# A run of four products per weight block, and retention's value products in runs of three key blocks

## Chip, cores and metric

The kernel runs on one core of one Trainium2 chip. The metric is the device time in microseconds (us) of one launch; its median over three runs is 3030.82 (3021.84 to 3036.25).

## What is computed

Two blocks of a network over 512 latent tokens and 256 context tokens, 1024 features each, in float32. The first block has two layers; the change touches the first layer's mixer, which is retention (eight heads of 64) beside a state-space scan. Two pieces matter here, in the reference's words.

Parameters of the modulation, from two conditioning vectors:

```
def adaln_params(cond, w_ada, b_ada):
    m = jax.nn.silu(cond) @ w_ada + b_ada
    return jnp.split(m[:, None, :], 6, axis=-1)
```

`w_ada` is 1024 x 6144. Retention, per head and direction, is a decayed attention without a softmax:

```
scores = jnp.einsum('bhnid,bhnjd->bhnij', qc, kc) * decay
y_intra = jnp.einsum('bhnij,bhnjv->bhniv', scores, vc)
```

with the state carried from chunk to chunk, forward and backward, and the latent scans starting from the context's final state. The kernel computes the same sum in one go: all 768 keys against the 512 latent queries, and the 256 context keys against the 256 context queries, each score multiplied by a decay that is a function of the distance.

## The kernel before

One program in Python emits instructions through helpers (`act` is line 382, `tt` line 390, `stt` line 393, `load` line 405), and a scheduler then sets each engine's order: of what is ready by its model it takes what stands first in the program, or in a high-priority block. SBUF is an arena whose places are taken in the order of their last release; PSUM is eight banks. All loads and spills are issued on one queue, SP, in order. The engines also work in order.

**Parameter products.** `ada(parts, w)` is called in this stage with parts 1 and 2 and w = 1. Each part is 2048 columns, in eight blocks of 128 rows of the weights. A block is four loads of 128 x 512 (256 KB each), and four products: the 32-column stationary operand holds the conditioning vectors, padded from two columns to 32, and product q writes PSUM partitions 32q to 32q + 32 of one bank (line 611). Each product follows its load, and the load's place is given back. The arena's zone 2 is 2560 floats a partition, five such places. After eight blocks come a copy, four transposes (line 620) and the sums with the bias.

**Retention.** `ret_pair` handles two heads. It first prepares `kk`, `qh` and `ql` (high and low parts of keys and queries; 64 x 768 pieces on ACT, DVE and POOL) and the decay strips `st` and `st2`. Then six key blocks J of 128: `scores` makes two products for each head (lines 1111 and 1112, 128 keys by 512 latent queries, 256 context queries too for J of 0 and 1) and multiplies them on DVE by the strip into `w`; `values` follows at once with one product per head (line 1120), 64 columns of stationary values, head i into partitions 64i to 64i + 64. The generator yields after each key block, seven times in all. `gn_center` (line 1168) and the statistics (line 1179) end the pair.

**The weave.** `mixer0` runs generators side by side: three head pairs (rate 27), the block gemms `blocks` (rate 8: the queries and keys of pairs 2 and 3, then four gate blocks; lines 435, 437 and 440), and `ada` (rate 18). Each step taken adds 1/rate to a generator's clock and the one that is furthest behind goes next; this sets the order in the program. A second weave holds the other mixer's finish (`ssd_finish`, rate 5) and the fourth pair (rate 9). After it come the norm's statistics (line 473), the finish's products and the output projection.

Float products (lines 611, 1120, 976, 1168) are two matmul instructions each in the trace; products of split operands (435, 437, 440, 1111, 1112) are one.

Of the kernel before, what the change touches and what calls it, by code (L numbers as in the profile page):

```python
# [12 lines left out]
OP = mybir.AluOpType  # L13
# [3 lines left out]
TL, TC, TA = 512, 256, 768  # L17
# [343 lines left out]
class _K:  # L361
# [19 lines left out]
    def act(self, out, in_, func=AF.Copy, **kw):  # L381
        return self.nc.scalar.activation(out, in_, func, **kw)  # L382

    def behind(self, ins, other):

        self.tc.add_manual_dep(ins.ins, other.ins.name, mybir.DependencyInfo(mybir.DependencyClass.Sync, mybir.DependencyReason.DATA),
                               reason="in one run")

    def tt(self, out, a, b, op, eng=None):
        return (eng or self.nc.vector).tensor_tensor(out, a, b, op=op)  # L390
# [208 lines left out]
    def ada(self, parts, w=2):  # L599

        nc, A, B = self.nc, self.A, self.B
        src, cs, out = self.I["wada"], self.cs, self.P[0]
        for g in parts:
            b = B.new()
            for k in range(8):
                for hf in range(4 // w):
                    c0 = g * 2048 + hf * w * 512
                    raw = self.load(src[k * 128:(k + 1) * 128, c0:c0 + w * 512])
                    for j in range(w):
                        q = w * hf + j  # L610
                        nc.tensor.matmul(b.a[32 * q:32 * q + 32, :], cs.a[:, k, :], raw.a[:, j * 512:(j + 1) * 512],  # L611
                                         start=(k == 0), stop=(k == 7))
                    raw.free()
                yield
            s = A.new([512])
            self.act(s.a, b.a)
            b.free()
            b2 = B.new()
            for nb in range(4):
                nc.tensor.transpose(b2.a[:, nb * 128:(nb + 1) * 128], s.a[:, nb * 128:(nb + 1) * 128], self.ident.a)  # L620
            s.free()
            src2 = b2.a.rearrange("p (n j v) -> p j n v", n=4, j=4)
            for v in range(2):
                self.tt(out.a[:, g * 16:(g + 1) * 16, v].rearrange("p (j n) -> p j n", j=4), src2[:, :, :, v],
                        self.bada.a[:, 0, g * 16:(g + 1) * 16].rearrange("p (j n) -> p j n", j=4), OP.add)
            b2.free()
            for q0 in (8, 32):
                if g * 16 <= q0 < g * 16 + 16:
                    nc.vector.tensor_scalar(out.a[:, q0:q0 + 8, :], out.a[:, q0:q0 + 8, :], 1.0, None, op0=OP.add)
# [442 lines left out]
    def ret_pair(self, c, pr, q, k, v):  # L1072

        nc, A, B = self.nc, self.A, self.B
        mm = nc.tensor.matmul
        la, lb, t, dst = c["la"], c["lb"], c["t"], c["dst"]
        half = [slice(0, 64), slice(64, 128)]
        if c["var"] is None:
            c["var"] = B.new()
        pyc, pvar = c["var"].a[:, :TC], c["var"].a[:, TC:TC + 48]  # L1080

        kk, qh, ql = (A.new([2, TA], F32R) for _ in range(3))
        for i in range(2):
            o, w = half[i], half[1 - i]
            self.act(kk.a[o, i, :], k.a[o])
            self.act(qh.a[o, i, :], q.a[o])
            self.act(qh.a[w, i, :], q.a[o])
            self.tt(kk.a[w, i, :], k.a[o], kk.a[o, i, :], OP.subtract, nc.gpsimd)
            self.tt(ql.a[o, i, :], q.a[o], qh.a[o, i, :], OP.subtract, nc.gpsimd)
            self.tt(ql.a[w, i, :], q.a[o], qh.a[o, i, :], OP.subtract)  # L1090
        self.free([k, q])
        st, st2, u = A.new([2, 896]), A.new([2, 640]), A.new([640])
        for i in range(2):
            h = 2 * pr + i
            nc.vector.tensor_scalar(st.a[:, i, :], dst.a, la.a[:, h:h + 1], None, op0=OP.mult)
            self.stt(st.a[:, i, :], dst.a, lb.a[:, 0, 8 + h:9 + h], st.a[:, i, :], OP.mult, OP.min)
            self.act(st2.a[:, i, :], dst.a[:, 256:896], AF.Exp, scale=la.a[:, h:h + 1], bias=lb.a[:, 1, h:h + 1])
            self.act(u.a, dst.a[:, 256:896], AF.Exp, scale=lb.a[:, 0, 8 + h:9 + h], bias=t.a[:, 8 + h:9 + h])
            self.tt(st2.a[:, i, :], st2.a[:, i, :], u.a, OP.add, nc.gpsimd)
        self.act(st.a, st.a, AF.Exp)  # L1100
        u.free()
        yield
        pyl = B.new()

        def scores(J, t0, t1, strip):
            n = t1 - t0
            p, w = B.new(2 if n > 256 else 1), A.new([2, n])
            p3 = p.a.rearrange("p (i t) -> p i t", i=2)
            js = slice(J * 128, (J + 1) * 128)
            for i in range(2):  # L1110
                mm(p3[:, i, :], kk.a[:, i, js], qh.a[:, i, t0:t1], start=True, stop=False)
                mm(p3[:, i, :], kk.a[:, i, js], ql.a[:, i, t0:t1], start=False, stop=True)  # L1112
            self.tt(w.a, p3, strip, OP.mult)
            p.free()
            return w

        def values(J, w, out, last):
            for i in range(2):
                vv = v.a[:, J, 128 * pr + 64 * i:128 * pr + 64 * i + 64]
                mm(out[half[i]], vv, w.a[:, i, :], start=(J == 0), stop=(J == last))  # L1120
            w.free()

        for J in range(6):
            if J < 2:
                strip = st2.a[:, :, 128 - 128 * J:640 - 128 * J]
            else:
                strip = st.a[:, :, 384 - 128 * (J - 2):896 - 128 * (J - 2)]
            values(J, scores(J, TC, TA, strip), pyl.a, 5)
            if J < 2:
                values(J, scores(J, 0, TC, st.a[:, :, 384 - 128 * J:640 - 128 * J]), pyc, 1)  # L1130
            yield
        self.free([st, st2, kk, qh, ql])
        yb = A.new([TA])
        self.act(yb.a[:, :TC], pyc)
        self.act(yb.a[:, TC:], pyl.a)
        pyl.free()
        self.dump("yret%d" % pr, yb.a)
        c["ds"].append(self.gn_center(yb, TA, c["center"], c["blk2"], pvar, pr))
# [1613 lines left out]
```

## Time and profile before

| what | value |
|---|---|
| median of three runs | 3030.82 us |
| profiled execution, its own time | 3028.96 us |
| its span | 3027.3 us, 43733 instructions |
| PE | 2845.5 us busy (94%), 17880 matmuls |
| DVE | 1704.7 us (56%) |
| ACT | 980.8 us (32%) |
| POOL | 298.6 us (10%) |
| line 611 | 1% of the chain that ended last |

A busy share is the time that an engine had an instruction under way. Matmuls are pipelined: one lasts longer than the distance to the next one's start, and several on separate strips of the array can be under way together, so lengths add up to more than busy time. In a timeline the distance from one start to the next start is what a piece of work takes from PE. The stage of this change lies between 290 and 460 us of the span.

### The profile page before, as it was taken

How to read it: one execution, taken by the hardware profiler on the slowest of the kernel's cores; microseconds unless marked ns; L12 is line 12 of the kernel's file. 1: busy time of each engine (PE TensorE's matmuls, PEld its weight loads, DVE VectorE, ACT ScalarE, POOL GpSimd, SP SyncE). 2: the span in 40 equal slices, each digit the busy share in tenths (PEclk: the TensorE clock that was granted, in tenths of full speed). 3: DMA queues.
4: the chain of work that ended last, by engine and by line, in shares of the span. 5: the costliest groups of instructions: out<-in, count | busy, mean ns of one | idle time of the engine just before them, and what ended most of it. 6: DMA issues, size and time to landing. Idle time of an engine off the chain costs nothing.

```text
span 3027.3 us, 43733 instructions
## 1 busy us (share of the span) xinstructions
PE 2845.5 (94%) x17880; PEld 2061.2 (68%) x17880; DVE 1704.7 (56%) x2733; ACT 980.8 (32%) x1605; POOL 298.6 (10%) x271
## 2 busy tenths in 40 slices
PE   7989999999999999999999999979799898999997
PEld 4776557888888877666698778876675664344443
DVE  5856447776576355677664782378856843121113
ACT  5522434511211146444554522254323322001011
POOL 0134310000000010122000000010311211000000
PEclk9999999999999999999999999989898888999998
DMA  6334362366465112001322222222213145999998
GB/s 220 104 108 122 122 196 76 119 212 218 140 223 202 42 66 93 21 31 42 118 70 91 91 77 77 71 84 77 71 49 105 43 147 207 398 409 409 409 409 294
DMA packets 170584, 458.98 MB, mean 152 GB/s; under 512 B 20320, under 2 KB 52704, under 8 KB 170000
## 3 DMA queue, kind: packets, MB, share of 16 engines
q1 hardware_dynamic: 170384, 456.19, 42.9%
q8 instruction: 140, 2.29, 0.3%
q14 instruction: 60, 0.49, 0.0%
HBM read 441.35 MB, written 14.78 MB: 151 GB/s over the span
## 4 chain that ended last, share of the span: by engine, by line
PE 68%; DVE 10%; DMA 5%; issue 4%; ACT 2%; POOL 1%; SPq 0%; DVEq 0%; ACTq 0%; POOLq 0%
PE ps L435 13%; PE ps L440 13%; PE ps L437 13%; PE ps L2609 9%; DVE mem L390 5%; ACT mem L382 2%; PE ps L2592 2%; PE ps L1625 1%; DVE mem L393 1%; DMA mem<-in_wadt_dram 1%; PE ps L611 1%; DMA mem<-in_ed_dram 1%; DMA mem<-in_eu_dram 1%; PE ps L1783 1%; POOL mem L390 1%
## 5 line engine op out<-in xcount | busy, mean ns | idle before, releaser
L382 ACT ACTIVATE mem<-mem 128x1024 fp32r<-128x1024 f32 (+16 forms) x802 | 543.2, 707 | 874.4 <-PE ps L440 223.3
L390 DVE TENSOR_TENSOR mem<-mem,mem 128x1024 fp32r<-128x1024 f32 (+13 forms) x595 | 507.9, 870 | 366.6 <-ACT mem L382 161.4
L382 ACT ACTIVATE mem<-ps 128x512 f32<-128x512 f32 (+8 forms) x607 | 311.9, 528 | 992.2 <-PE ps L440 334.4
L435 PE MATMUL ps<-mem,mem 128*128 128x512 f32 (+3 forms) x1991 | 597.3, 357 | 14.9 <-ACT mem L382 10.8
L437 PE MATMUL ps<-mem,mem 128*128 128x512 f32 (+2 forms) x1906 | 568.5, 354 | 1.1 <-DVE mem L390 0.9
L440 PE MATMUL ps<-mem,mem 128*128 128x512 f32 (+2 forms) x1977 | 417.6, 352 | 0.0
L435 PEld LDWEIGHTS ps<-mem,mem 128*128 128x128 f32 (+2 forms) x1991 | 338.2, 189 | 82.8 <-ACT mem L382 17.8
L437 PEld LDWEIGHTS ps<-mem,mem 128*128 128x128 f32 (+1 forms) x1906 | 325.6, 189 | 60.8 <-issue 6.7
L440 PEld LDWEIGHTS ps<-mem,mem 128*128 128x128 f32 (+1 forms) x1977 | 324.1, 190 | 56.2 <-issue 4.1
L2609 PE MATMUL ps<-mem,mem 128*64 128x512 f32 x1344 | 309.5, 599 | 1.1 <-ACT mem L382 0.3
L437 PE MATMUL ps<-mem 128*128 128x512 f32 (+1 forms) x814 | 272.5, 365 | 1.4 <-POOL mem L390 0.9
L435 PE MATMUL ps<-mem 128*128 128x512 f32 (+1 forms) x729 | 255.1, 374 | 12.4 <-ACT mem L382 8.5
L390 POOL TENSOR_TENSOR mem<-mem 128x256 f32<-128x256 f32 (+4 forms) x72 | 96.2, 1337 | 1683.5 <-ACT mem L382 1392.8
L390 DVE TENSOR_TENSOR mem<-mem,ps 128x512 f32<-128x512 f32 (+5 forms) x234 | 129.0, 582 | 203.5 <-PE ps L2609 103.5
L2609 PEld LDWEIGHTS ps<-mem,mem 128*64 128x64 f32 x1344 | 107.2, 137 | 177.9 <-issue 163.8
L390 DVE TENSOR_TENSOR mem<-mem 128x256 f32<-128x256 f32 (+19 forms) x347 | 186.4, 544 | 68.6 <-ACT mem L382 22.9
L390 POOL TENSOR_TENSOR mem<-mem,mem 128x512 f32<-128x512 f32 (+6 forms) x104 | 142.5, 1380 | 534.4 <-ACT mem L382 438.0
L390 DVE TENSOR_TENSOR mem<-ps,mem 128x512 f32<-128x512 f32 (+6 forms) x196 | 123.1, 644 | 99.1 <-PE ps L1112 35.2
L437 PEld LDWEIGHTS ps<-mem 128*128 128x128 f32 x814 | 152.8, 195 | 27.9 <-DVE mem L390 2.5
L440 PE MATMUL ps<-mem 128*128 128x512 f32 (+3 forms) x743 | 171.4, 360 | 0.0
L435 PEld LDWEIGHTS ps<-mem 128*128 128x128 f32 x729 | 139.2, 196 | 44.8 <-ACT mem L382 13.4
L393 DVE SCALAR_TENSOR_TENSOR mem<-ps,mem 128x256 f32<-128x256 f32 (+1 forms) x232 | 114.6, 533 | 76.2 <-PE ps L440 75.9
(301 smaller groups left out, 2901.7 us busy)
## 6 DMA issues: line engine op xcount, KB each, us to landing
mem<-in_eg_dram SPq DMA_DIRECT2D x128, 512.0 KB, 10.2
mem<-in_eu_dram SPq DMA_DIRECT2D x128, 512.0 KB, 10.2
mem<-in_ed_dram SPq DMA_DIRECT2D x128, 512.0 KB, 10.2
mem<-in_wadt_dram SPq DMA_DIRECT2D x96, 512.0 KB, 4.3
mem<-in_wup_dram SPq DMA_DIRECT2D x44, 512.0 KB, 3.6
mem<-in_wgate_dram SPq DMA_DIRECT2D x44, 512.0 KB, 3.5
mem<-in_wdown_dram SPq DMA_DIRECT2D x40, 512.0 KB, 3.5
mem<-in_w2in_dram SPq DMA_DIRECT2D x35, 512.0 KB, 3.6
```

Of the source, the lines that this page charges most:

```text
L382: return self.nc.scalar.activation(out, in_, func, **kw)
L390: return (eng or self.nc.vector).tensor_tensor(out, a, b, op=op)
L393: return self.nc.vector.scalar_tensor_tensor(out, a, s, b, op0=op0, op1=op1)
L435: mm(o, w(0, k), acts[k][0][:, ts], start=(k == 0), stop=False)
L437: mm(o, w(0, k), acts[k][1][:, ts], start=False, stop=False)
L440: mm(o, w(1, k), acts[k][0][:, ts], start=False, stop=(k == nk - 1))
L611: nc.tensor.matmul(b.a[32 * q:32 * q + 32, :], cs.a[:, k, :], raw.a[:, j * 512:(j + 1) * 512], start=(k == 0), stop=(k == 7))
L1625: m = mm(po.a[64 * i:64 * i + 64, :], v.a[:, kb, 64 * h:64 * h + 64], pt.a[:, i, :], start=(kb == 0), stop=(kb == 5))
L1783: self.nc.tensor.matmul(out, src, i, start=True, stop=True)
L2592: mm(b.a[:, :256], ht.a[:, c, fs], o, start=(c == 0), stop=(c == 3))
L2609: mm(bk.a[64 * i:64 * i + 64, 512 * n:512 * n + 512], lhs(k, i), w[i][:, 512 * n:512 * n + 512], start=(k == 0), stop=(k == 7))
```

## The change

`ada` loads the four pieces of a block first, then issues its four products in a high-priority block, from q = 3 down to 0, the last three placed behind the first in PE's order, without a semaphore. `behind` gets a parameter for that. `ret_pair` makes the scores of three key blocks, with a yield after each, and then all their products with the values in a high-priority block, each waiting for the run's last multiplication; then it yields again, which makes nine yields for a pair.

```
-    def behind(self, ins, other):
-
-        self.tc.add_manual_dep(ins.ins, other.ins.name, mybir.DependencyInfo(mybir.DependencyClass.Sync, mybir.DependencyReason.DATA),
-                               reason="in one run")
+    def behind(self, ins, other, how=mybir.DependencyClass.Sync):
+
+        self.tc.add_manual_dep(ins.ins, other.ins.name, mybir.DependencyInfo(how, mybir.DependencyReason.DATA), reason="in one run")
...
-                for hf in range(4 // w):
-                    c0 = g * 2048 + hf * w * 512
-                    raw = self.load(src[k * 128:(k + 1) * 128, c0:c0 + w * 512])
-                    for j in range(w):
-                        q = w * hf + j
-                        nc.tensor.matmul(b.a[32 * q:32 * q + 32, :], cs.a[:, k, :], raw.a[:, j * 512:(j + 1) * 512],
-                                         start=(k == 0), stop=(k == 7))
-                    raw.free()
+                raw = [self.load(src[k * 128:(k + 1) * 128, c0:c0 + w * 512]) for c0 in range(g * 2048, g * 2048 + 2048, w * 512)]
+
+                with self.tc.high_priority():
+                    first = None
+                    for q in range(3, -1, -1):
+                        m = nc.tensor.matmul(b.a[32 * q:32 * q + 32, :], cs.a[:, k, :], raw[q // w].a[:, q % w * 512:q % w * 512 + 512],
+                                             start=(k == 0), stop=(k == 7))
+                        if first:
+                            self.behind(m, first, mybir.DependencyClass.NoSync)
+                        first = first or m
+                self.free(raw)
                 yield
...
-            self.tt(w.a, p3, strip, OP.mult)
+            e = self.tt(w.a, p3, strip, OP.mult)
             p.free()
-            return w
-
-        def values(J, w, out, last):
-            for i in range(2):
-                vv = v.a[:, J, 128 * pr + 64 * i:128 * pr + 64 * i + 64]
-                mm(out[half[i]], vv, w.a[:, i, :], start=(J == 0), stop=(J == last))
-            w.free()
-
-        for J in range(6):
-            if J < 2:
-                strip = st2.a[:, :, 128 - 128 * J:640 - 128 * J]
-            else:
-                strip = st.a[:, :, 384 - 128 * (J - 2):896 - 128 * (J - 2)]
-            values(J, scores(J, TC, TA, strip), pyl.a, 5)
-            if J < 2:
-                values(J, scores(J, 0, TC, st.a[:, :, 384 - 128 * J:640 - 128 * J]), pyc, 1)
+            return w, e
+
+
+        for J0 in range(0, 6, 3):
+            run = []
+            for J in range(J0, J0 + 3):
+                if J < 2:
+                    strip = st2.a[:, :, 128 - 128 * J:640 - 128 * J]
+                    run.append((J, scores(J, 0, TC, st.a[:, :, 384 - 128 * J:640 - 128 * J]), pyc, 1))
+                else:
+                    strip = st.a[:, :, 384 - 128 * (J - 2):896 - 128 * (J - 2)]
+                run.append((J, scores(J, TC, TA, strip), pyl.a, 5))
+                yield
+            with self.tc.high_priority():
+                for J, (w, _), out, last in run:
+                    for i in range(2):
+                        vv = v.a[:, J, 128 * pr + 64 * i:128 * pr + 64 * i + 64]
+                        self.behind(mm(out[half[i]], vv, w.a[:, i, :], start=(J == 0), stop=(J == last)), run[-1][1][1])
+            for _, (w, _), _, _ in run:
+                w.free()
             yield
```

## Rows read from the trace of the kernel before

**Rows 1.** Busy us of each engine by stretch, granted clock, DMA share, GB/s.

```profile
290.00:442.00 152.00, 150.29 (x723) 85.60 (x722) 70.05 (x69) 55.06 (x68) 42.70 (x24) 1.00 0.48 157
340.00:350.00 10.00, 9.22 (x55) 5.11 (x54) 6.70 (x7) 2.68 (x4) 3.26 (x2) 1.00 0.50 159
430.00:440.00 10.00, 10.00 (x49) 6.21 (x48) 1.98 (x2) 5.59 (x7) 3.72 (x3) 1.00 0.77 256
442.00:460.00 18.00, 15.13 (x70) 7.28 (x70) 14.58 (x19) 5.56 (x7) 0.85 (x1) 1.00 0.59 179
460.00:480.00 20.00, 18.19 (x71) 13.24 (x69) 12.75 (x25) 14.36 (x20) 0.00 (x0) 0.66 0.58 187
```

**Rows 2.** Chain of waits, 290 to 442 us, shares by line.

```profile
by line: PE ps L611 19.9%; PE ps L435 14.0%; PE ps L437 13.8%; PE ps L1120 13.5%; PE ps L440 13.5%; PE ps L1111 7.9%; PE ps L1112 6.3%; POOL mem L390 2.9%; PE ps L1179 2.6%; PE ps L976 2.1%; PE ps L1168 1.8%; DVE mem L390 0.8%; ACT mem L382
```

**Rows 3.** Timeline of PE, 319 to 326 us: start, length, instruction, count.

```profile
319.47 1.06 PE L611 MATMUL ps<-mem 128*32 128x512 f32 x6
320.46 0.50 PE L1111 MATMUL ps<-mem,mem 128*128 128x512 f32 x1
320.80 0.40 PE L1112 MATMUL ps<-mem,mem 128*128 128x512 f32 x1
321.03 0.40 PE L1111 MATMUL ps<-mem,mem 128*128 128x512 f32 x1
...
322.19 0.39 PE L1112 MATMUL ps<-mem,mem 128*128 128x512 f32 x1
322.51 1.04 PE L611 MATMUL ps<-mem 128*32 128x512 f32 x2
323.49 1.94 PE L1120 MATMUL ps<-mem,mem 128*64 128x512 f32 x8
325.36 1.05 PE L611 MATMUL ps<-mem 128*32 128x512 f32 x4
```

**Rows 4.** Timeline of PE, 346 to 350 us.

```profile
346.76 1.51 PE L1120 MATMUL ps<-mem,mem 128*64 128x512 f32 x8
348.21 1.06 PE L611 MATMUL ps<-mem 128*32 128x512 f32 x8
349.20 0.50 PE L1111 MATMUL ps<-mem 128*128 128x512 f32 x1
```

**Rows 5.** Timeline of PE, 427 to 434 us.

```profile
427.24 1.90 PE L611 MATMUL ps<-mem 128*32 128x512 f32 x10
429.07 0.62 PE L435 MATMUL ps<-mem,mem 128*128 128x256 f32 x2
...
433.05 1.05 PE L611 MATMUL ps<-mem 128*32 128x512 f32 x2
```

**Rows 6.** Timeline of PE, first and last group of line 611.

```profile
291.40 1.04 PE L611 MATMUL ps<-mem 128*32 128x512 f32 x2
...
436.92 1.05 PE L611 MATMUL ps<-mem 128*32 128x512 f32 x2
```

**Rows 7.** Timeline of PE, 459.8 to 461 us.

```profile
459.83 1.08 PE L1120 MATMUL ps<-mem 128*64 128x512 f32 x4 [1.60 <-DVE mem L390]
460.84 0.38 PE L473 MATMUL ps<-mem 128*128 128x1 f32 x2
```

**Rows 8.** Waits, weight loads of PE, 290 to 442: total us, times, longest.

```profile
PEld ps L611 <- DMA mem<-in_wada_dram: 0.4, 1, 0.4
```

**Rows 9.** Timeline of SP's issues, 428 to 430 us.

```profile
428.32 1.36 SPq L405 DMA_DIRECT2D mem<-in_wada_dram  x3
```

**Rows 10.** DMA issues, 290 to 442: count, KB each, median us to landing.

```profile
mem<-in_wada_dram SPq DMA_DIRECT2D x59, 256.0 KB, 3.5
```

**Rows 11.** Timeline of ACT, 410 to 420 us.

```profile
413.57 3.44 ACT L382 ACTIVATE mem<-mem 64x768 fp32r<-64x768 f32 x4 [1.51 <-PE ps L1112]
```

**Rows 12.** Timeline of POOL, 420 to 435 us.

```profile
429.86 1.81 POOL L390 TENSOR_TENSOR mem<-mem,mem 64x768 fp32r<-64x768 f32 x1 [5.03 <-ACT mem L382]
```

**Rows 13.** Timeline of PE, 440 to 443 us.

```profile
442.83 0.48 PE L1111 MATMUL ps<-mem,mem 128*128 128x512 f32 x1
```

## The prediction

> **What bounds the kernel now.** I looked first at the busy time by stretch, because the change touches one stage only: the weave of retention, the block gemms and the parameter products, from 290 to 442 us, and the short weave behind it, 442 to 460. [rows 1] show the matmul engine busy for 150.29 of 152 us in the first of these at the full granted clock (1.00, 2.4 GHz); DVE has 70, ACT 55 and POOL 43 of the 152. From 442 to 460 PE has 15.13 of 18 and DVE 14.58: there both matter. From 460 to 480 the granted clock is 0.66, a mixture of 1.2 and 2.4 GHz, behind that less busy stretch.
>
> Second, the chain of waits of the first stretch [rows 2]: nearly all of it is PE. L611 (the parameter products) holds 19.9% of the 152 us, 30.2 us; L1120 (retention's products with the values) 13.5%, 20.5 us. POOL has 2.9%, DVE 0.8%. So PE time saved there moves the end of the stage, and no other engine is near taking its place.
>
> Third, the timeline of PE, read from start to next start. In [rows 3] six instructions of L611 take 0.99 us (319.47 to 320.46) and two take 0.98 (322.51 to 323.49); in [rows 4] eight take 0.99 (348.21 to 349.20). A float product is two instructions here, so up to four products on the four 32-column strips run side by side at the price of one. What costs is the number of groups, not of products. [rows 5] have the longest: ten instructions in 1.83, one group and a second.
>
> **The change part by part.** The sum is made against the profiled execution's own 3028.96 us (span 3027.3 and 1.66 around it); the median of the three runs, 3030.82, lies 1.86 above.
>
> *A. Parameter products in runs.* The 64 products (128 instructions) now form 31 uninterrupted groups: 15 of two instructions, 6 of four, 4 of six, 5 of eight, 1 of ten (the first at 291.40, the last at 436.92 [rows 6]). Start to next start they take 15 x 0.98 + 6 x 0.98 + 4 x 0.99 + 5 x 0.99 + 1.83 = 31.3 us. Afterwards the other three products of a block wait in PE's order for the one whose load came last, so each of the 16 blocks is one group of eight: 16 x 0.99 = 15.9. Saved: 15.4.
>
> A rule weighed: the eight of [rows 4] cost what the two of [rows 3] cost, 0.99 against 0.98. The Trainium skill, "TensorE: Matmul & The Clock Gate", section "Part 3: Packing small matmuls — row/col tiling", gives only 2.38x for three column tiles; four at that efficiency would be 3.17x, an estimate from that page, a group would take 1.24, and A would save 11.5 instead of 15.4. The measured group has all four, so 0.99 stands.
>
> *B. Values in runs.* Two 64-column halves run side by side as well. A pair of 512 columns alone takes 1.01 (459.83 to 460.84 [rows 7]); two pairs take 1.87 (323.49 to 325.36 [rows 3]), so a further one costs 0.86, and a pair of 256 columns 0.44 (the stretch of 1.45 from 346.76 in [rows 4] holds one of each). Now there are 23 uninterrupted stretches (one of them at 323.49 [rows 3], the last at 459.83 [rows 7]) of 27.6 us in all, start to next start. Afterwards each head pair has two: 3 x 0.86 + 2 x 0.44 + 0.15 and 3 x 0.86 + 0.15, together 6.3; four head pairs, 25.3. Saved: 2.3. The same products, weights and multiplications stay; only their order moves.
>
> *C. Fewer changes of tile shape.* Score products follow each other at 0.23 (320.80 to 321.03). The last one ahead of a narrow group takes 0.32 (322.19 to 322.51), the first one behind it 0.34 (320.46 to 320.80) [rows 3]: 0.09 and 0.11 more. PE enters narrow work from wide work 42 times now, at most 24 times afterwards (16 + 8). Saved: 18 x 0.20 = 3.6.
>
> A to C make 21.3. The last head pair lies behind 442, where PE waits for DVE; its share (0.8 of B; 5 entries of C, 1.0) I count as nothing. That leaves 19.5 in the stretch that PE bounds.
>
> *D. The loads, and the wait that they add.* A block's products used to start as each 256 KB piece landed; now all four wait for the last one. The zone has five places of 512, so three of the next block's four loads wait on SP for the run before; behind them on SP stand the gemms' weights and the spills. Behind the run on PE, which works in order, stands everything. Lower bound: no cost; in all 31 groups of today PE waited 0.4 us for this tensor [rows 8], and loads issued from 428.32 on [rows 9] are used from 433.05 on [rows 5], 4.7 later, against a median landing of 3.5 [rows 10]. Upper bound: where the placing allows for a lone load only, three more in line at the stretch's 256 GB/s [rows 1] bring the fourth 3 x 1.02 = 3.1 late; 15 blocks, 46 us. I take 1.0, close to the row of 0.4.
>
> *E. The re-spaced steps.* A head pair yields 9 times instead of 7 while its rate stays 27 for three. The last scores of the third pair come at 25/27 = 0.93 of the weave instead of 20/27 = 0.74; the last gate block stays at 7/8 = 0.88. Today the fourth pair's preparation (ACT, POOL and DVE on the buffers that the third pair frees) runs from 413.57 [rows 11] to 431.67 (429.86 and 1.81 [rows 12]), 18.1 us, hidden below two gate gemms, and its first scores start at 442.83 [rows 13], when the gemms end. Afterwards the last scores may stand behind the last gemm, and only 8 x 0.23 of scores and 2.7 of values are left to cover the preparation. Upper bound: 18.1 - 4.6 = 13.5. Below nothing: the pair's work can fall into PE's idle 2.9 us of 442 to 460 and 1.8 of 460 to 480 [rows 1], where PE waits for the other mixer's finish, so up to -2. The nearest row is the start of the second pair, whose preparation stood in front of its first scores at 340: 0.8 us of idle PE (9.22 of 10 [rows 1]). I take 1.0. The values of the last run also wait for the third multiplication; that lies in the same place and is in this term.
>
> *F. Nothing.* The ACT, DVE and POOL instructions stay the same in number and size; held weights need more SBUF, the deeper order costs no instruction.
>
> Sum: 19.5 - 1.0 - 1.0 = 17.5 us; 3028.96 - 17.5 = 3011.5, and with 1.86 to the median 3013.3. Behind 480 the stages are the same and move up as they are.
>
> **The rivals.**
> *The fourth pair comes late* (E near its upper bound). For: 18.1 us of preparation, steps moved behind the last gate block. Against: the other mixer's finish and its projection are independent work. A to C less 11: 8 saved, 3022 on the median.
> *The runs wait for their fourth load* (D near its upper bound), the case on the other side. One mechanism: a place for only one load ahead, four loads in one burst behind the run that frees their places, and PE standing in order in front of the run. For: SP is one queue, and the loads cannot start earlier. Against: 0.4 us of waiting today, and a block has 150/16 = 9.4 us. It eats the gain from 19.5/15 = 1.3 us per block on and makes the kernel slower by over 0.5% from 2.3; at the full 3.1 it is 46 - 18.5, 3058.
> *The runs don't form*: other ready work still comes between, or the loads of a block straddle gemms as they do today. A shrinks to a third; 3024.
>
> **How the numbers follow.** Forecast 0.62; late fourth pair 0.18; late loads 0.15; no runs 0.05. The runs of the kernel before lie up to 0.5% apart (15.2 us), about what a measurement can tell from no change. The forecast's own range is 3003 to 3023; two thirds of its chance lie beyond 15.2 us of gain, that is below 3015.7: 0.41 faster, 0.21 within. The late pair gives 0.03 faster and 0.15 within, the late loads 0.14 slower and 0.01 within, no runs 0.05 within. Faster 0.44, within 0.5% 0.42, slower 0.14. The range for 8 in 10 takes in the late pair, the missing runs and the mildest late loads: 3001 to 3034.
>
> **What would show it.** Right: L611 in about 16 groups of eight with 16 to 17 us busy; L1120 in eight stretches; the last gate gemm ends near 423 instead of 442, and PE is still busy over 97% before that; PE waits for the parameter loads stay at a few us. E is right if the first scores of the fourth pair follow the last gemm within some 5 us. I am wrong if PE shows waits for the parameter loads of 1 us and more ahead of most runs (D), if PE idles 10 us between the last gemm and the fourth pair (E), or if the stage ends 20 us earlier and the end does not.

## The result, and the profile after

The changed kernel is slower: 3065.41 us median of four runs (3058.43 to 3070.50) against 3027.02 (3021.84 to 3036.25) of the kernel before in the same session; ratio 1.0121 [1.0099, 1.0143]. The forecast was 3013, with a range up to 3034. The profiled execution took 3058.43 us, 29.5 more than that of before, with a span of 3056.7. It is the fastest of the four, so the traces can explain 29.5 of the 38.4 us between the medians. In it PE is busy for 2839.8 us (93%), DVE for 1709.1, ACT for 984.4 and POOL for 297.1, all within 6 us of before.

In the new listing the lines have moved: the parameter products are line 610, the scores 1113 and 1114, the values 1134, the block gemms 434, 436 and 439; 382 is ACT's helper, 389 that of `tt`, 404 the load, 472 the norm that begins behind the tail.

Two landmarks serve throughout, both read from PE's timeline: the end of the last gate gemm (line 439; 442.6 us before) and the start of the finish's norm (line 472; 460.8 before). Between them lies what I call the tail, 18.2 us before. After the change they stand at 458.9 and 502.3, the tail is 43.4. So 16.3 us are lost ahead of the last gate gemm and 25.2 in the tail, 41.5 in all; at the end of the profiled executions 29.5 of that are left.

First the busy time by stretch (columns as in [rows 1]).

```profile
282.00:459.00 177.00, 153.16 (x754) 95.44 (x746) 60.40 (x65) 45.59 (x59) 39.31 (x22) 0.96 0.37 120
350.00:370.00 20.00, 15.10 (x61) 11.04 (x59) 10.52 (x10) 5.03 (x6) 4.77 (x3) 0.74 0.16 52
360.00:365.00 5.00, 5.00 (x20) 4.05 (x17) 0.51 (x1) 0.34 (x1) 0.00 (x0) 0.50 0.58 186
430.00:440.00 10.00, 8.25 (x43) 6.78 (x44) 2.74 (x3) 1.90 (x2) 1.07 (x1) 0.97 0.02 7
470.00:490.00 20.00, 14.04 (x52) 7.61 (x51) 13.07 (x14) 14.41 (x17) 4.35 (x3) 0.66 0.45 135
490.00:510.00 20.00, 10.24 (x41) 4.93 (x39) 12.40 (x20) 11.28 (x15) 0.00 (x0) 0.72 0.49 159
```

Where PE idled 1.71 of 152 us [rows 1], it now idles 23.84 of 177. The stage was bound by PE; it no longer is. From 430 to 440, where PE had no gap and all DMA together moved 256 GB/s [rows 1], PE has 8.25 us and DMA 7 GB/s: the last parameter products start at 416, and nothing of that kind is left to fill in. PE's busy time did shrink, to 153.16 us, some of it at a low clock, against 158.89 from 282 to 442.6 before. Not all of that is saved: the third pair's last run of values (463.55 to 467.79) now falls behind the window.

The chain of waits from 282 to 459 us says what took PE's place. The first line groups it, those below are pieces in order of time (start, length, what).

```profile
by line: DMA mem<-in_wada_dram 26.4%; PE ps L610 13.0%; PE ps L434 9.9%; PE ps L436 9.4%; DVE mem L389 6.6%; SPq L404 5.4%; PE ps L439 4.9%; PE ps L1134 4.1%; POOL mem L389 2.8%; PE ps L1114 2.7%; PE ps L1113 2.7%; PE ps L1185 2.2%; DVE mem
...
288.64 1.19 PE ps L610 x8
291.09 4.18 DMA mem<-in_wada_dram
295.31 1.06 PE ps L610 x8
297.71 4.00 DMA mem<-in_wada_dram
301.75 1.06 PE ps L610 x8
```

In [rows 2] no DMA is named; here the loads of the parameters' weights head the list with 26.4% of 177 us. The pieces form a cycle: run, load, run. A run gives its places back, the load that is needed last starts to move 1.4 us later (the run that began at 288.64 ends at 289.7, the piece of DMA begins at 291.09), lands 4 us after that, and the next run starts at once. PE's timeline shows the same from PE's side; the bracket is the idle time ahead and what ended it.

```profile
281.69 1.06 PE L610 MATMUL ps<-mem 128*32 128x512 f32 x8
288.64 1.07 PE L610 MATMUL ps<-mem 128*32 128x512 f32 x8 [1.32 <-DMA mem<-in_wada_dram]
295.31 1.06 PE L610 MATMUL ps<-mem 128*32 128x512 f32 x8 [1.17 <-DMA mem<-in_wada_dram]
301.75 1.06 PE L610 MATMUL ps<-mem 128*32 128x512 f32 x8 [0.80 <-DMA mem<-in_wada_dram]
308.54 1.07 PE L610 MATMUL ps<-mem 128*32 128x512 f32 x8 [1.56 <-DMA mem<-in_wada_dram]
316.06 1.07 PE L610 MATMUL ps<-mem 128*32 128x512 f32 x8 [1.79 <-DMA mem<-in_wada_dram]
325.35 1.07 PE L610 MATMUL ps<-mem 128*32 128x512 f32 x8 [1.30 <-DMA mem<-in_wada_dram]
...
358.75 1.88 PE L610 MATMUL ps<-mem 128*32 128x512 f32 x8 [4.10 <-DVE mem L389]
...
364.15 0.63 PE L434 MATMUL ps<-mem,mem 128*128 128x512 f32 x1
364.57 0.63 PE L436 MATMUL ps<-mem,mem 128*128 128x512 f32 x1
```

The runs are there, eight instructions in 1.06 us as in [rows 4]. But they stand 6.4 to 7.5 us apart for the first six, the pace of the loads, and not the 9.4 that I had divided out. At 358.75 the first run of the second part waits 4.10 us more, for a PSUM bank that small sums on DVE have to release. The granted clock of 350 to 370 is 0.74 in the mean; behind the gap, from 360 to 365, it is 0.50, the lower of the two levels, and wide products follow each other at 0.42 (364.15 to 364.57) instead of 0.23 [rows 3].

The sums of PE's waits, 282 to 459 us (total, times, longest), where before PE's products had none for the loads and its weight loads 0.4 [rows 8]; the weight loads' waits are 18.4 now:

```profile
PE ps L610 <- DMA mem<-in_wada_dram: 11.6, 10, 1.8
PE ps L610 <- DVE mem L389: 4.1, 1, 4.1
PE ps L1114 <- POOL mem L389: 2.5, 2, 1.7
PE ps L1113 <- DVE mem L389: 2.3, 3, 1.3
```

The tail, PE's timeline, two rows of POOL's and one of DVE's:

```profile
458.75 0.40 PE L1113 MATMUL ps<-mem 128*128 128x512 f32 x1
...
463.55 1.08 PE L1134 MATMUL ps<-mem,mem 128*64 128x512 f32 x4 [3.02 <-DVE mem L389]
...
467.79 0.52 PE L1113 MATMUL ps<-mem,mem 128*128 128x256 f32 x1
...
479.60 0.79 PE L1113 MATMUL ps<-mem,mem 128*128 128x512 f32 x1 [3.24 <-DVE mem L389]
...
497.05 3.68 PE L1134 MATMUL ps<-mem,mem 128*64 128x512 f32 x8 [4.83 <-DVE mem L389]
...
500.51 1.88 PE L1134 MATMUL ps<-mem 128*64 128x512 f32 x4
502.32 1.50 PE L472 MATMUL ps<-mem 128*128 128x1 f32 x12
```

```profile
459.61 4.29 POOL L389 TENSOR_TENSOR mem<-mem,mem 64x768 fp32r<-64x768 f32 x2 [16.04 <-PE ps L1114]
...
476.75 1.53 POOL L389 TENSOR_TENSOR mem<-mem 128x640 f32<-128x640 f32 x1 [5.76 <-ACT mem L382]
...
478.32 1.22 DVE L389 TENSOR_TENSOR mem<-ps,mem 128x1024 f32<-128x1024 f32 x1 [2.88 <-POOL mem L389]
```

The fourth pair's last decay strip on POOL, before:

```profile
439.49 1.57 POOL L390 TENSOR_TENSOR mem<-mem,mem 128x640 f32<-128x640 f32 x1 [4.92 <-ACT mem L382]
```

The third pair's last scores are now behind the last gate gemm (458.75), so the high and low parts of the fourth pair's keys and queries, which were done on POOL at 431.67 before [rows 12], are done at 463.90, and its first scores stand at 467.79 instead of directly behind the gemm [rows 13]: 8.9 us late. From there to the norm it takes 34.5 us instead of 18.0, for three reasons that the rows show. The pair's last decay strip ends on POOL at 478.28 (before at 441.06, ahead of the gate gemm's end), DVE's multiplication by it waits for that, and the next scores on PE wait 3.24 us for DVE (479.60). The last values wait for a multiplication that DVE makes last (4.83 us ahead of 497.05). And PE runs at 0.66 to 0.72 of its clock in a stretch where it is half idle, so those eight instructions take 3.46 to the next start (500.51), where [rows 3] have 1.87.

### The profile page after: what moved, and what is told of

It is laid out like the page before. It is cut to its first block, busy times and chain, and to the rows that moved or that the text cites. A ratio compares the mean times of both kernels' runs of the same rounds, so it can differ in the third digit from the quotient of the medians.

```text
span 3056.7 us, 43748 instructions
## 1 busy us (share of the span) xinstructions
PE 2839.8 (93%) x17880; PEld 2061.3 (67%) x17880; DVE 1709.1 (56%) x2733; ACT 984.4 (32%) x1607; POOL 297.1 (10%) x271
## 4 chain that ended last, share of the span: by engine, by line
PE 65%; DVE 12%; DMA 6%; issue 4%; ACT 3%; POOL 1%; SPq 1%; DVEq 0%; ACTq 0%; POOLq 0%
PE ps L434 13%; PE ps L436 13%; PE ps L439 12%; PE ps L2615 9%; DVE mem L389 6%; ACT mem L382 3%; PE ps L2598 2%; DVE mem L392 2%; DMA mem<-in_wada_dram 2%; PE ps L1631 1%; POOL mem L389 1%; DMA mem<-in_wadt_dram 1%; DMA mem<-in_eu_dram 1%; PE ps L1789 1%; PE ps L610 1%
## 5 line engine op out<-in xcount | busy, mean ns | idle before, releaser
L389 DVE TENSOR_TENSOR mem<-mem,mem 128x1024 fp32r<-128x1024 f32 (+19 forms) x597 | 509.9, 870 | 413.7 <-ACT mem L382 169.6
L389 POOL TENSOR_TENSOR mem<-mem 128x512 f32<-128x512 f32 (+4 forms) x75 | 98.9, 1320 | 1632.4 <-ACT mem L382 1382.7
L389 DVE TENSOR_TENSOR mem<-mem 128x256 f32<-128x256 f32 (+22 forms) x345 | 182.9, 538 | 73.9 <-ACT mem L382 28.9
L389 DVE TENSOR_TENSOR mem<-ps,mem 128x512 f32<-128x512 f32 (+5 forms) x196 | 123.3, 644 | 100.7 <-PE ps L1114 34.5
```

## The experiments

Seven edits were combined. Undoing the values' part gives `ada_*` kernels, undoing the parameters' part gives `val_*`, `full_*` and `both_*` have both parts. "Session" means kernels timed beside the same runs of the kernel before. Landmarks are written as last gate gemm / norm / tail.

**1. Each part alone.** In `ada_only` retention is as before:

```
-            e = self.tt(w.a, p3, strip, OP.mult)
+            self.tt(w.a, p3, strip, OP.mult)
...
-        for J0 in range(0, 6, 3):
...
+        for J in range(6):
...
+            values(J, scores(J, TC, TA, strip), pyl.a, 5)
```

> The parameter products in runs alone; retention as before. Theory W (the loss has two halves: high-priority runs wait in PE's order for their fourth load and for a bank, and the re-spaced pair steps push the third and fourth head pair behind the last gate gemm): the runs keep their waits (11.6 us for loads, 4.1 for the bank in the changed kernel) against 15 to 19 us saved, so 3020 to 3035. Rival V (all of the loss is retention's): 3005 to 3014. Rival R (all of the loss is the runs'): 3055 to 3070.

Measured: 3050.59 us (3037.67 to 3056.34), 1.0061 [1.0039, 1.0083]; 460.9 / 478.7 / 17.8. The tail is as before, the stage ahead of it is as late as in the whole change, and the waits repeat:

```profile
PE ps L610 <- DMA mem<-in_wada_dram: 10.5, 13, 2.1
PE ps L434 <- DVE mem L991: 4.2, 1, 4.2
```

So the parameters' part alone gives the loss ahead of the last gemm, without retention's.

In `val_only` the loop over `hf` with its loads and products is as before:

```
-                with self.tc.high_priority():
-                    first = None
-                    for q in range(3, -1, -1):
...
+                for hf in range(4 // w):
...
+                    raw.free()
```

> The values in runs of three key blocks with nine yields alone; the parameter products as before. Theory W: no load waits, the last gate gemm ends within 5 us of before, and the stretch from its end to the finish's norm statistics grows from 18 to some 35 to 45 us: 3035 to 3055. Rival V: 3055 to 3070. Rival R: 3018 to 3028.

Measured: 3053.26 (3048.93 to 3057.02), 1.0067 [1.0047, 1.0087]; 444.6 / 491.2 / 46.6. The last gate gemm stands almost where it did, the tail has the whole loss. PE's busy time in the tail (15.13 of 18 us in [rows 1]) and its waits there:

```profile
444.60:491.00 46.40, 29.74 (x105) 14.69 (x103) 32.02 (x36) 22.43 (x28) 9.84 (x5) 0.71 0.43 141
```

```profile
PE ps L1131 <- DVE mem L389: 10.5, 2, 6.0
PE ps L1110 <- DVE mem L389: 4.3, 4, 2.6
```

Each part is slower by itself, and 0.61% and 0.67% add to about the 1.21% of the whole.

**2. The yields.** One yield less in each run of three, seven for a pair as before:

```
-                yield
+                if J < J0 + 2:
+                    yield
```

> The whole change, but the yield after the third key block's scores is left out, so a pair takes seven steps as before. Theory W: the third pair is done ahead of the last gate gemm again, the stretch behind it is 18 to 25 us; the load waits stay at 10 to 15 us: 3025 to 3045. Rival V': the spacing is no matter, the runs of three themselves cost the time (values wait for the third multiplication): 3055 to 3070.

Measured: 3058.54 (3048.44 to 3062.33), 1.0084 [1.0061, 1.0107]; 472.0 / 489.0 / 17.0. The time missed the expectation and lies in the rival's range. The tail is cured completely, but the last gate gemm is 13 us later than in the whole change, the waits for the loads rise from 11.6 to 14.5 us and the clock of 282 to 472 is 0.92.

The same edit on the values' part alone:

> The values' runs alone, with seven yields for a pair. Theory W (the re-spaced steps cost retention's half): the stretch from the last gate gemm to the finish's norm statistics falls from 46.6 us (nine yields) to 18 to 24, and the time to 3022 to 3034. Rival V' (runs of three cost the time by themselves, since the values wait for the third multiplication): 3045 to 3056.

Measured: 3037.52 (3032.14 to 3042.04), 1.0036 [1.0021, 1.0051]; 450.0 / 467.7 / 17.7. The time lies between the two expected ranges. The yields' number does set the tail; half of `val_only`'s loss stays with seven yields. The parameter products, left as in the kernel before, now fall into 34 groups of 36.4 us instead of 31 of 31.3, and PE idles 5.35 of the 160 us from 282 to 442 instead of 1.71.

**3. The priority of the parameter products.** They take their turn in the program instead:

```
-                with self.tc.high_priority():
+                if True:
                     first = None
```

> The whole change, but the four parameter products of a block stand at the program's own priority (still one behind the first in PE's order). Theory W: PE's waits for the parameter loads fall from 11.6 to under 3 us and the last gate gemm ends 10 to 15 us earlier than in the changed kernel; the stretch behind it stays at 35 to 45 us: 3045 to 3058. Rival L: not the priority but the four loads in one burst make the wait: waits stay near 11 us and the time at 3060 to 3070.

Measured: 3045.33 (3043.03 to 3050.56), 1.0048 [1.0032, 1.0064]; 438.8 / 484.5 / 45.7. Waits for the loads fall from 11.6 to 6.3, not to under 3 as expected, and the stage ends 20 us earlier ahead of an uncured tail.

> The parameter products' runs alone, at the program's own priority. Theory W (priority puts the run in front of PE before its loads have landed): PE's waits for the parameter loads fall from 10.5 us to under 5 and the last gate gemm ends ahead of 442: 3015 to 3030. Rival L (four loads in one burst into five places are late at any priority): waits of 8 us and more, 3040 to 3055.

Measured: 3024.98 (3016.25 to 3033.99), 0.9991 [0.9975, 1.0007]; 443.9 / 462.5 / 18.6. The waits are 3.6 us in three places, and the 16 blocks are 16 groups of 15.9 us, the number of step A to the tenth. From `ada_only` to this kernel only the priority changes, and the loss of 0.61% is gone. But the last gate gemm is not earlier than before: the 15.4 us that the products give are spent as idle PE, 11.0 of 161.9 us.

**4. Places for the loads.** Zone 2 gets eight places of 512 instead of five:

```
-        A.reserve(2, 2560)
+        A.reserve(2, 4096)
```

> The parameter products' runs alone, with high priority, and eight places for the loads instead of five, so that a whole block can be on its way during a run. Rival L: the waits fall under 3 us, 3012 to 3028. Theory W: the run is still put where the scheduler's model has the loads landed, waits of 7 us and more stay, 3035 to 3052.

Measured: 3033.02 (3022.68 to 3039.14), 1.0014 [0.9997, 1.0031]; 452.4 / 470.0. With the priority kept, places for two blocks cut the waits for the loads from 10.5 to 3.7 us and the loss to nothing that can be told; the time lies between the two expected ranges, and the gain expected of the runs is not there. PE waits on DVE, ACT and POOL instead (4.2 for line 991, 3.0, 2.8, 2.6).

> Both halves with what theory W holds to be their costs taken away: seven yields, the program's own priority, eight places. Theory W: 3010 to 3026, load waits under 4 us, the stretch behind the last gate gemm 18 to 24 us. If the two halves cost by something else: 3035 and more.

Measured: 3020.56 (3015.44 to 3027.57), 0.9976 [0.9964, 0.9989]; 448.8 / 467.4. With all three cures both parts together are 0.24% faster than before, though the stage itself ends 6.6 us later: that gain arises behind it, and I did not trace it further.

> The kernel before with eight places for the parameter loads instead of five, nothing else. If the best version so far owes its 7 us to the runs: 3024 to 3031, no difference. If it owes them to the places: 3015 to 3022.

Measured: 3018.74 (3013.41 to 3024.81), 0.9979 [0.9968, 0.9989]; 433.0 / 455.2. The places help the kernel before too. Its loads run further ahead: the last one is issued at 407.2 us and the last group stands at 421.0, 13.8 later; with five places these are 429.2 and 436.9, 7.7. Its products fall into 20 groups of 20.9 us instead of 31. Two thirds of what step A was to save on PE come without any run, 10.4 us, and 0.21% of the time, 6 us, with them.

**5. The loads taken away.** Only the first block's four loads of the stage are made, all later blocks use them again; so 60 of the 64 loads fall away:

```
-                raw = [self.load(src[k * 128:(k + 1) * 128, c0:c0 + w * 512]) for c0 in range(g * 2048, g * 2048 + 2048, w * 512)]
+                if g == parts[0] and k == 0:
+                    raw = [self.load(src[k * 128:(k + 1) * 128, c0:c0 + w * 512]) for c0 in range(g * 2048, g * 2048 + 2048, w * 512)]
...
-                self.free(raw)
+                if g == parts[-1] and k == 7:
+                    self.free(raw)
```

> Runs at the program's priority alone; 60 of the 64 parameter loads are left out, all blocks use the first block's four pieces. Theory Q (the 15 us saved on PE come back as waits because SP, in order, holds the gemms' weight loads and the spills behind parameter loads that wait for a run): the last gate gemm ends at 422 to 432 instead of 444, 3005 to 3018. Rival P (the head pairs' preparation on ACT, DVE and POOL is the next bound): it ends at 438 to 446, 3018 to 3030.

Measured: 3012.42 (3005.47 to 3027.45), 0.9953 [0.9936, 0.9971]; 428.5 / 451.1. 16 groups, 15.9 us, clock 1.00 from 282 to 428.5. With no load to wait for, the parameters' part is worth 14.7 us, and the last gate gemm moves by 14.1: near A's 15.4, seen in the time at last.

> The whole change with high priority and nine yields; 60 of the 64 parameter loads are left out. Theory W: no load waits, so the last gate gemm ends 12 to 25 us earlier than in the changed kernel, at 434 to 447; the stretch behind it stays at 40 to 46 us; 3038 to 3053. Rival: the waits at the runs were only a place where PE waited for something else: 3058 to 3068.

Measured: 3044.37 (3042.05 to 3045.62), 1.0061 [1.0046, 1.0076]; 436.1 / 481.0 / 44.9. Against the whole change (1.0121) the loads cost 0.60%, 18 us. The stage still ends with the long tail.

**6. The cures together, first without places.**

> Both halves with seven yields at the program's own priority, five places as in the change. If the places matter as little as theory W has it once the priority is gone: 3018 to 3030. If they make the version with eight: 3030 to 3045, with 5 us and more of waits for the parameter loads.

Measured: 3045.06 (3039.09 to 3050.54), 1.0063 [1.0045, 1.0082]; 454.7 / 473.9. No better than `full_nohp` (1.0048), although the norm starts 10.6 us earlier in the trace; the two profiled executions do differ by 11.5 us (3050.56 and 3039.09), the medians do not. The waits for the loads are 10.1 us in five places; `ada_nohp`, without the values' runs, has 3.6.

> The whole change with seven yields and without 60 of the 64 parameter loads: both costs that theory W and Q name are taken away, and the runs stay. If the prediction's terms A to C (21 us less PE work) were right and only its terms D (loads) and E (spacing) were mis-sized: the last gate gemm ends 12 to 20 us ahead of before, 3005 to 3017. If a saving in PE's work is not worth its time here, or the values' runs cost by themselves: 3022 to 3040.

Measured: 3048.66 (3038.40 to 3053.82), 1.0065 [1.0041, 1.0088]; 464.5 / 484.2. This was to settle that loads and yields are all, and it missed by over 30 us: no loads, seven yields, and still as slow as `full_noload`. The trace says why. PE's timeline has all runs of both parts early:

```profile
282.13 7.08 PE L611 MATMUL ps<-mem 128*32 128x512 f32 x64
...
316.19 7.05 PE L611 MATMUL ps<-mem 128*32 128x512 f32 x58
```

and behind them PE idles (320 to 464.5 us):

```profile
320.00:464.50 144.50, 123.63 (x588) 86.48 (x581) 66.73 (x65) 55.22 (x67) 42.44 (x22) 0.89 0.20 64
```

20.9 us idle and a clock of 0.89, with waits on DVE, POOL and ACT, which prepare the pairs. High priority with nothing to wait for spends in 41 us the work that would have filled PE's waits in the 140 us behind.

> Both halves with seven yields, the parameter products at the program's own priority and without 60 of the 64 loads. Theory F (with high priority all 16 runs are done by 316 us and nothing is left to fill PE while retention prepares; that, not the runs, made the last kernel without loads slow): the parameter runs are spread to 410 us again, PE idles under 6 us up to the last gate gemm, which ends at 420 to 432: 3005 to 3017. Rival V' (the values' runs of three cost by themselves): 3025 to 3042.

Measured: 3028.86 (3016.08 to 3037.67), 0.9999 [0.9981, 1.0018]; 439.6 / 457.9. The same kernel with the parameter products at program priority: the runs last until 402 us, PE idles 10.8 us behind 320 at a clock of 0.99, and the time is 20 us lower. So the priority costs 20 us with no loads in play, shown by one edit; that the used-up filler is how is the reading of the two traces. It is not all, though: the time expected from that reading was 3005 to 3017, the measured one lies in the rival's range, and `ada_nohp_noload`, which differs by the values' runs alone, is 0.46% faster, 14 us.

**7. Places once more.**

> The change as it is with eight places for the parameter loads instead of five. The loads cost the change 21 us (with and without them); if five places are most of that, 3045 to 3055 and load waits under 5 us; if the priority is, they stay above 8 us and the time at 3056 to 3068.

Measured: 3058.50 (3052.23 to 3065.47), 1.0102 [1.0075, 1.0129]; 448.3 / 491.2 / 42.9. The places alone take the waits for the loads from 11.6 to 2.2 us, and the time falls by 7 us only, within the intervals and above the range expected for so few waits: the tail stays, the 4.1 us at the PSUM bank stay, the clock is 0.92 from 282 to 448.3.

> The parameter products' runs at the program's priority with eight places, retention as before: the version that the runs so far point to. Theory Q: places for two blocks let the loads run ahead, the last gate gemm ends at 426 to 434, 3010 to 3020, that is at or below the kernel before with eight places (3018.7). If runs add nothing once there are places: 3018 to 3028.

Measured: 3012.86 (3007.98 to 3019.33), 0.9952 [0.9937, 0.9968]; 430.4 / 454.2. With all loads made it is as fast as the kernel with 60 of them left out. It beats the kernel before by 14 us and, by the two ratios, the changed one by some 50. Of the 14 us the eight places alone give 6 (`before_8s`, 0.9979); the runs add 0.27%, 8 us, with intervals that touch. Against `ada_8s` (1.0014), which differs by the priority alone, it is 0.62% faster, 19 us, though the waits for the loads differ by 2.2 us only. With the priority the last run stands at 346.9, without it at 419.2, and PE idles 18.65 us of the stage instead of 5.5:

```profile
282.00:452.40 170.40, 151.75 (x785) 95.39 (x786) 75.97 (x76) 60.62 (x74) 47.88 (x26) 0.98 0.44 144
```

That is the priority's cost once more, with all loads made. Three runs of `ada_nohp_8s`:

```profile
291.45 1.07 PE L610 MATMUL ps<-mem 128*32 128x512 f32 x8
...
319.91 1.06 PE L610 MATMUL ps<-mem 128*32 128x512 f32 x8
335.23 1.06 PE L610 MATMUL ps<-mem 128*32 128x512 f32 x8
...
```

No idle time stands ahead of them; PE waits for the loads 1.5 us in all, and from 282 to the last gate gemm it is busy for 142.89 of 148.4 us at the full clock:

```profile
282.00:430.40 148.40, 142.89 (x769) 90.98 (x768) 74.49 (x72) 57.64 (x73) 47.84 (x25) 1.00 0.49 161
```

> The same with twelve places, three blocks' worth. Theory Q: within 4 us of the one with eight, 3010 to 3020; if eight places still hold the loads back, 4 us and more below it.

Measured, with 6144 in place of 4096: 3013.11 (3004.78 to 3017.23), 0.9950 [0.9933, 0.9967]; 435.8 / 456.0. Places for three blocks add nothing to those for two.

**8. The priority of the values' runs,** the last suspect for what they cost by themselves:

```
-            with self.tc.high_priority():
+            if True:
                 for J, (w, _), out, last in run:
```

> The values' runs alone with seven yields, at the program's own priority; each product still waits for the third multiplication. If the priority makes the 10 us that they cost: 3022 to 3030. If the wait for the third multiplication or the broken-up parameter products (34 groups) make them: 3033 to 3045.

Measured: 3040.61 (3038.29 to 3048.65), 1.0047 [1.0032, 1.0061]; 458.8 / 480.3. Not better than `val_7y` (1.0036), so the priority is not it. The parameter products again fall into 34 groups, of 38.6 us, and PE idles 6.3 us from 282 to 442.

## Why the prediction was wrong, step by step

**What bounds the stage.** "PE time saved there moves the end of the stage, and no other engine is near taking its place" is true of the kernel before and was taken to hold for any order of the same work. It does not: PE works in order, and the change decides what stands in front of it. Nearly one to one it held in two settings: `ada_nohp_noload` (14.1 us in the stage, 14.7 in the time) and `ada_nohp_8s` (12.2 and 14.3), although at the norm the gain is only 9.7 and 6.7 and the rest comes behind it. With five places the same 15.9 us of products gave 2.7 us, which is within the noise (`ada_nohp`).

**A held in size, not in worth.** 16 groups, 15.9 us, in `ada_nohp` to the digit. With the high priority there are 21 groups of 21.6 us, low clock and waits included.

**B held in size too:** 26.0 us in nine stretches in `val_7y`, 25.3 in eight foreseen; in the changed kernel there are 12 stretches of 38.1, waits and low clock included. It was never seen as a gain. With seven yields, values' runs cost time in all five pairs of kernels that differ by them: 0.36% (`val_7y`), 0.46% (no loads), 0.72% (five places), and, with intervals that overlap, 0.24% (eight places) and 0.23% (five places, with the priority). Part of it is shown in `val_7y`: the parameter products break into 34 groups (5.1 us) and PE idles 3.6 us more. The wait for the third multiplication is not seen there: PE waits 4.4 us for DVE ahead of values up to the norm, 3.8 before; but no run took that wait away. The rest stays open.

**C held in count.** Up to the norm PE enters narrow work from wide work 24 times, the bound that was set, instead of 42. What an entry costs could not be told from the waits and the clock.

**D was mis-sized, the first of the two steps of the sum that failed.** 1.0 us was put there; PE waits 11.6 us for these loads, and without them the change is 18 us faster (`full_noload`). Eight places took 9.4 us of the waits away and gave 7 us (`full_8s`); what makes up the rest of the 18 is not shown. My upper end, 46 us, held it, and the rival of late loads described it: "a place for only one load ahead, four loads in one burst behind the run that frees their places, and PE standing in order in front of the run". I argued against it with 0.4 us of waiting before and 9.4 us for a block. Both were numbers of another order: single products had been placed behind their loads, and nothing holds blocks 9.4 us apart when a high priority lets a run go ahead of all other ready work. The runs show both halves: priority off takes the loss of `ada_only` away (1.0061 to 0.9991), eight places do most of it (1.0014), and the two together give the gain (0.9952). At the full change the waits lie at 0.8 to 1.8 us a run, below the 2.3 from which I had the rival make the kernel slower; alone they would have eaten 11.6 of A's 15.4 us, not more.

**E was mis-sized beyond its bound.** 1.0 taken, 13.5 the upper end, 25.2 measured in the tail. The reasoning about the place was right: the third pair's last scores fell behind the last gate gemm, and the fourth pair's preparation lost its cover. The 18.1 us of preparation in the bound left out the decay strips, although the scores' products cannot be used without them: before, the last strip ends at 441.06, 27.5 us behind the start at 413.57, and with that the bound's own sum gives 22.9 (an estimate, as ACT did other work in between). Also left out was what comes behind: a pair alone at the end waits for DVE's multiplications ahead of scores (6.0 us) and of its last run of values (4.83), and PE half idle runs at 0.66 to 0.72 of its clock. The late start is 8.9 us, below the bound; the slower pair is 16.5 more. With seven yields the tail is 17.0 to 21.4 us in all kernels. In the time they give less than in the tail: 0.37% (`after` to `full_7y`) and 0.31% (`val_only` to `val_7y`), some 10 us, with intervals that just overlap. That nothing comes out in two other pairs (`full_nohp` against `both_7y_nohp`, 1.0048 and 1.0063; `full_noload` against `full_noload_7y`, 1.0061 and 1.0065) can in the second pair be laid to the used-up filler; in the first the traces agree with the profiled executions and not with the medians, and it stays open.

**F, "nothing", hid the priority.** I treated it as what makes the runs form. It also moves the parameter products forward, and the work that PE could do while pairs are prepared is then missing: 20 us between `full_noload_7y` and `both_7y_nohp_noload`, with no loads in play, and 19 between `ada_8s` and `ada_nohp_8s`, with all of them. In the changed kernel the loads hold the runs back, the last one to 416 us (the last group stood at 436.9 before), and how much of that cost it carries is not shown.

**"Behind 480 the stages are the same and move up as they are"** failed the other way: the shift is 49 us at the first broadcast behind the norm (477.6 to 526.6), 43 by 600, 33 by 1040, 40 at 1280 and 30 at the end of the profiled execution. One stretch that gives some back is this, before and, 49 us later, after:

```profile
700.00:800.00 100.00, 94.97 (x536) 82.70 (x535) 56.75 (x93) 20.75 (x25) 0.00 (x0) 0.97 0.49 163
```

```profile
749.00:849.00 100.00, 100.00 (x576) 87.90 (x576) 67.96 (x113) 20.09 (x25) 0.00 (x0) 1.00 0.59 200
```

Where PE idled 5 us before, it has no gap after and gets more instructions done (576 for 536). That a late PE finds ready what it used to wait for is my reading; no run tested it.

## What to carry to other kernels

Grouping products into runs pays only if their operands can be there before the run's turn: count the places for the next run's loads (two blocks' worth here), and read the distance of the runs against the time of place, issue and landing. Do not give high priority to work that waits for a burst of loads, nor to filler: the first stops an in-order engine in front of it, the second spends early what was to cover other engines' work. When a generator gets more steps in a weave, list what falls behind the last piece of the longest other generator, and price that end with the clock that an idle PE is granted.

## What had not been expected of the hardware

Idle time on PE cost twice here. In stretches with gaps of 3 to 5 us the mean granted clock lay at 0.66 to 0.74, between the levels of 1.2 and 2.4 GHz (0.50, the lower one, from 360 to 365 us), and there products took nearly double: 0.42 us for a wide one instead of 0.23, 3.46 for two narrow pairs (eight instructions) instead of 1.87. And a transfer that an engine is hardly seen to wait for can still cost: in the kernel before PE's weight loads waited 0.4 us for these loads and its products not at all [rows 8], yet eight places instead of five moved its last gate gemm from 442.6 to 433.0 us. The last load was issued 13.8 us ahead of the last group instead of 7.7, and the products' groups went from 31 to 20; a group costs what one product costs (0.99 us for eight instructions, 0.98 for two).
